# Joining the inverse of the delta rule: both steps' products spread over column places of the matrix engine, copied out by halves

## The chip, the cores and the metric

The kernel runs on one core of a Trainium2 chip. The metric is the device time of one execution in microseconds (us); the median of three runs of the kernel before is 1582.2 us (1581.89 to 1582.7). TensorE (PE in the profile, PEld for its weight loads), VectorE (DVE), ScalarE (ACT), GpSimd (POOL) and the queues of SyncE (SP) run side by side and wait for each other by semaphores.

## The reference, cut to what matters

One layer of a hybrid decoder: 256 tokens, model width 2048, a wide input projection, two branches (a gated delta rule with 32 value heads and an mLSTM with 8 heads), two output projections, a merge and an output product. The change concerns the delta rule alone. For each head and each chunk of tokens it solves a unit lower triangular system:

```python
    lower = jnp.where(strict, jnp.einsum('nbhid,nbhjd->nbhij', k_beta, kc) * decay, 0.0)
    unit_lower = lower + jnp.eye(CHUNK, dtype=f32)
    rhs = jnp.concatenate([v_beta, k_beta * jnp.exp(g_cum)[..., None]], axis=-1)
    sol = lax.linalg.triangular_solve(unit_lower, rhs, left_side=True, lower=True, unit_diagonal=True)
```

The kernel uses token blocks of 128 instead of chunks of 64, and applies the inverse of the 128x128 triangle to the right hand side.

## The kernel before, in words

**The stream.** `Stream.run` (L95) walks through all weights in pieces of 128x1024 numbers. A piece is cast by ScalarE into a high part (`whi`, L173), VectorE subtracts for the low part (`wlo`, L174), and TensorE multiplies both with the activations (L235, L628, L632). Up to three pieces are prepared ahead of their use (`ahead`, L67). After each piece used, `Side.step` (L46) lets every side job issue one step, in order of rank; a side job is a generator, and each `yield` in it hands back to the stream. So TensorE's program alternates between a piece of weights and what the side jobs add behind it. `side.debt` is a planner's account of VectorE time: a step takes off 1.6, jobs add their cost or give a credit where they put work on TensorE, and `side.room` (L53) holds the base inverse back while the account is too full.

**A period.** The delta rule has eight periods, `zg` 0 to 7 (`gdn_period`, L1039). Each one handles four heads with two token blocks each, so eight triangles of 128x128, numbered `m`, with m = 2 x head + token block. `base_inverse` (L815) inverts the 32x32 blocks on the diagonals on VectorE and puts them into `x0` (inverses by partition) and `y0` (their transposes); `xcmp` and `ycmp` hold them compactly, eight blocks side by side in each quarter of the partitions. `gdn_stage2` (L869) joins them. It starts 31 steps behind its period's scores (`STAGE2_STEPS`), while the next period's weights stream.

**The first step of the joining** (L879 to L906) makes 64x64 inverses from 32x32 ones. For each `m` and each half `t` of the triangle (partitions `r` = 64t and `o` = 64t + 32) one 32x32 product goes into the bank `mp` (L886), is copied to `pc_` (L890), and a second product goes into `mx` (L897, L900): two for the lower half (the block and its transpose), one for the upper half. Copies with the sign turned take them to `y0` (L902) and `x0` (L905).

**The second step** (L908 to L950) does the same from 64 to 128, for eight `m`: `first` (L911) makes 64x64 products from partitions 0 to 63 into partitions 64 to 127 of the bank `mq`, which are copied to `p2` (L924, L933); `second` (L914) multiplies from partitions 64 to 127 into partitions 0 to 63 of the bank `mz`, copied to `x0` (L932, L949). It is issued in three side steps: the four even `m` of `first`; then the four odd `m` of `first` alternating with the four even of `second`; then, behind the four products `pa` (L944) that apply the even blocks' inverse, the four odd `m` of `second`.

**What follows**: `pa`, `pb`, `pc` and `po` (L944, L956, L966, L974 to L977) apply the inverse and form the outputs.

**Places.** A product reads its two operands from some partitions (its rows in the array) and writes to some partitions of a PSUM bank (its columns in the array). A product of 32 or 64 rows and columns takes only a part of the 128x128 array, which is called its place here; its row place is where its operands lie, its column place is where its output lies. PSUM banks are handed out in turn by `gtile` (L206), four of them for all side jobs; a job waits for the next one with `banks`.

Of the kernel before, what the change touches and what calls it, by code (L numbers as in the profile page):

```python
# [9 lines left out]
AF = mybir.ActivationFunctionType  # L10
# [5 lines left out]
P = 128  # L16
S = 256
# [101 lines left out]
def hybrid_layer_kernel(  # L119
# [25 lines left out]
    V, A, T, G, SP = nc.vector, nc.scalar, nc.tensor, nc.gpsimd, nc.sync  # L145
# [60 lines left out]
    def gtile(nm, held=False):  # L206
        i = slots[0] % 4
        slots[0] += 1
        t = pg.tile([P, 512], F32, name=nm, tag="g")
        freed[i] = 1 << 30 if held else side.t + 1  # L210
        slots[1][id(t)] = i, t
        return t

    def gfree(t):
        freed[slots[1].pop(id(t))[0]] = side.t

    def banks(n):

        while any(freed[(slots[0] + j) % 4] >= side.t for j in range(n)):
            yield  # L220
# [16 lines left out]
    side = Side()  # L237
# [468 lines left out]
    def wait(n):  # L706
        for _ in range(n):
            yield
# [106 lines left out]
    def base_inverse(zg, res, zr):  # L815
# [49 lines left out]
        while zg < 7 and side.t < res["t"] + STAGE2_STEPS - 1:  # L865
            yield
        side.add(gdn_stage2(zg, res, zr), 0)

    def gdn_stage2(zg, res, zr):  # L869

        au, xc, yc = [res["au", z] for z in range(2)], res["xcmp"], res["ycmp"]

        def um(m):
            return au[m // 4][:, m % 4 // 2, 256 + 384 * (m % 2):384 + 384 * (m % 2)]

        def cols32(t, n=0):
            return t[:, n:n + 256].rearrange("p (m i) -> p m i", m=8)

        pc_ = bp.tile([P, 8, 32], F32, name="pcm", tag="pcm", bufs=1)  # L879
        yield from banks(2)  # L880
        pss = [gtile(f"mp{t}", True) for t in range(2)]
        side.debt -= 0.6
        for m in range(8):
            for t in range(2):
                r, o = 64 * t, 64 * t + 32
                T.matmul(pss[t][o:o + 32, m * 32:(m + 1) * 32], um(m)[r:r + 32, o:o + 32], yc[r:r + 32, m],  # L886
                         start=True, stop=True)
        for t in range(2):
            o = 64 * t + 32
            A.copy(pc_[o:o + 32], cols32(pss[t])[o:o + 32])  # L890
            gfree(pss[t])
        yield
        yield from banks(2)
        psx = [gtile(f"mx{t}", True) for t in range(2)]
        side.debt -= 0.6
        for m in range(8):
            T.matmul(psx[0][32:64, S + m * 32:S + (m + 1) * 32], xc[32:64, m], pc_[32:64, m], start=True, stop=True)  # L897
            for t in (1, 0):
                r, o = 64 * t, 64 * t + 32
                T.matmul(psx[t][r:r + 32, m * 32:(m + 1) * 32], pc_[o:o + 32, m], xc[o:o + 32, m],  # L900
                         start=True, stop=True)
        A.activation(y0[32:64, :, 0:32], cols32(psx[0], S)[32:64], AF.Copy, scale=-1.0)  # L902
        for t in range(2):
            r = 64 * t
            A.activation(x0[r:r + 32, :, r + 32:r + 64], cols32(psx[t])[r:r + 32], AF.Copy, scale=-1.0)  # L905
            gfree(psx[t])  # L906
        yield from wait(1 + (zg == 6))
        p2 = bp.tile([P, 8, 64], F32, name="p2", tag="p2", bufs=1)  # L908

        def first(ps, j, m):  # L910
            T.matmul(ps[64:128, j * 64:(j + 1) * 64], um(m)[0:64, 64:128], y0[:, m], start=True, stop=True)  # L911

        def second(ps, j, m):
            T.matmul(ps[0:64, j * 64:(j + 1) * 64], p2[64:128, m], x0[64:128, m, 64:128], start=True, stop=True)  # L914

        def part64(ps, r, o):
            return ps[r:r + 64, o:o + S].rearrange("p (m i) -> p m i", m=4)

        yield from banks(1)
        psp = gtile("mq", True)  # L920
        side.debt -= 0.5
        for j in range(4):
            first(psp, j, 2 * j)
        A.activation(p2[64:128, 0:8:2], part64(psp, 64, 0), AF.Copy, scale=-1.0)  # L924
        yield
        yield from banks(1)
        psz = gtile("mz", True)
        side.debt -= 0.5
        for j in range(4):
            first(psp, 4 + j, 2 * j + 1)  # L930
            second(psz, j, 2 * j)
        A.copy(x0[0:64, 0:8:2, 64:128], part64(psz, 0, 0))  # L932
        A.activation(p2[64:128, 1:8:2], part64(psp, 64, S), AF.Copy, scale=-1.0)  # L933
        gfree(psp)
        yield

        rr = res["rr"].rearrange("p b z (h d) -> p b (z h d)", h=2)
# [1 line left out]
        heads = [(g, g // 2, g % 2, slice(g * P, (g + 1) * P)) for g in range(4)]  # L939
        yield from banks(1)  # L940
        pa = gtile("pa", True)
        side.debt -= 1.3
        for g, z, h, c in heads:
            T.matmul(pa[:, c], x0[:, 2 * g], rr[:, 0, c], start=True, stop=True)  # L944
        for j in range(4):
            second(psz, 4 + j, 2 * j + 1)
        A.copy(ys[:, 0], pa)
        gfree(pa)
        A.copy(x0[0:64, 1:8:2, 64:128], part64(psz, 0, S))  # L949
        gfree(psz)  # L950
        yield from wait(2)
        yield from banks(1)
        pb = gtile("pb", True)
# [583 lines left out]
```

## Time and profile before

| | |
|---|---|
| median of 3 runs | 1582.2 us (1581.89 to 1582.7) |
| the profiled execution's own time | 1583.33 us |
| its span, first to last instruction | 1581.6 us |
| PE busy | 1565.7 us (99%) |
| PEld busy | 1315.6 us (83%) |
| DVE busy | 1159.7 us (73%) |
| ACT busy | 967.2 us (61%) |
| POOL busy | 249.7 us (16%) |
| DMA | 372.22 MB, mean 235 GB/s |
| granted clock of TensorE | 0.998 |

Busy time is the time in which at least one instruction of the engine was under way. In the timeline rows that are shown below, the columns are the start in us, the length in us of the merged row, the engine, the line, the operation, output <- inputs, rows*columns of the array, the shape, the number of records, and in brackets how long the engine was idle ahead of it and what released it. A float32 product shows as two records of its line: the sixteen products of L886 in a period are `x32`. Records overlap, since products are pipelined, so a cost is read from the start of a row to the start of the next one.

### The profile page before, as it was taken

Reading aid. Unit: us, or ns where it says so; the run is one execution under the profiler, and the core shown is the slowest. Engines: PE = TensorE matmul, PEld = TensorE weight load, DVE = VectorE, ACT = ScalarE, POOL = GpSimd, SP = SyncE. Lnnn points to the kernel's source line nnn. Section 1 sums busy time; section 2 is a strip of 40 time slices with the busy share of each in tenths; the row PEclk is TensorE's granted clock in tenths of the full one; section 3 lists DMA queues with packets and bytes.
Section 4 is the critical chain, followed back from the end, with each engine's and each line's share of the span. In section 5 each row is a group of like instructions: output and inputs, shape, how many; then the busy total and the mean of one; then the engine's idle time right before and its main releaser. Section 6 shows DMA issues by size and latency. Waiting matters only on the chain.

```text
span 1581.6 us, 23140 instructions
## 1 busy us (share of the span) xinstructions
PE 1565.7 (99%) x8574; PEld 1315.6 (83%) x8574; DVE 1159.7 (73%) x1884; ACT 967.2 (61%) x1608; POOL 249.7 (16%) x204
## 2 busy tenths in 40 slices
PE   8999999999999999999999999999999999999997
PEld 5888888888888888888888888888888888888886
DVE  6785556865789887988887988775868766756654
ACT  7754446765666676767676776766666554544443
POOL 4787761000000000000000000000000000100100
PEclk9999999999999999999999999999999999999999
DMA  9998775975565646575656565647878878766572
GB/s 379 392 385 334 267 288 188 288 245 193 182 195 175 209 147 202 167 201 168 202 167 198 172 199 171 199 142 247 281 270 314 339 264 298 282 237 237 213 269 107
DMA packets 167739, 372.22 MB, mean 235 GB/s; under 512 B 26021, under 2 KB 127797, under 8 KB 140105
## 3 DMA queue, kind: packets, MB, share of 16 engines
q1 hardware_dynamic: 167240, 370.13, 67.6%
q8 instruction: 67, 1.10, 0.3%
q10 hardware_dynamic: 290, 0.53, 0.1%
q14 instruction: 46, 0.38, 0.1%
q0 software_dynamic: 96, 0.09, 0.0%
HBM read 354.40 MB, written 16.31 MB: 234 GB/s over the span
## 4 chain that ended last, share of the span: by engine, by line
PE 81%; issue 13%; ACT 2%; DMA 1%; DVE 1%; POOL 1%; DVEq 0%; SPq 0%; ACTq 0%; POOLq 0%
PE pn L235 36%; PE pt L628 19%; PE pt L632 9%; PE py L235 8%; POOL mg L1327 1%; ACT whi L173 1%; DMA ya<-o_dr 1%; PE psa L235 1%; PE mq L911 1%; PE csil L305 0%; PE po L977 0%; PE pc L966 0%; PE po L976 0%; PE po L974 0%; PE pb L956 0%
## 5 line engine op out<-in xcount | busy, mean ns | idle before, releaser
L174 DVE TENSOR_TENSOR wlo<-raw,whi 128x1024 fp32r<-128x1024 f32 x453 | 556.1, 1235 | 241.1 <-ACT whi L173 240.2
L173 ACT CAST whi<-raw 128x1024 fp32r<-128x1024 f32 x516 | 532.1, 1046 | 261.3 <-PE pn L235 133.2
L235 PE MATMUL pn<-whi,h 128*128 128x512 f32 x1792 | 563.7, 392 | 0.9 <-ACT part L478 0.6
L628 PE MATMUL pt<-h,whi 128*128 128x512 f32 x1280 | 408.5, 400 | 0.0
L235 PEld LDWEIGHTS pn<-whi,h 128*128 128x128 f32 x1792 | 336.4, 188 | 71.9 <-ACT part L478 1.5
L235 PE MATMUL pn<-wlo,h 128*128 128x512 f32 x896 | 349.1, 390 | 0.9 <-POOL wlo L174 0.9
L632 PEld LDWEIGHTS pt<-h,wlo 128*128 128x128 f32 x1280 | 240.4, 188 | 56.6
L632 PE MATMUL pt<-h,wlo 128*128 128x256 f32 x1280 | 252.1, 278 | 0.0
L235 PEld LDWEIGHTS pn<-wlo,h 128*128 128x128 f32 x896 | 168.4, 188 | 35.4 <-POOL wlo L174 1.7
L628 PEld LDWEIGHTS pt<-h,whi 128*128 128x128 f32 x1280 | 195.4, 189 | 2.4
L174 POOL TENSOR_TENSOR wlo<-raw,whi 128x1024 fp32r<-128x1024 f32 (+1 forms) x63 | 145.7, 2320 | 51.6 <-ACT whi L173 51.6
L235 PE MATMUL py<-whi,yhi 128*128 128x512 f32 x384 | 150.8, 393 | 0.0
L235 PE MATMUL py<-whi,ylo 128*128 128x512 f32 x384 | 149.7, 390 | 0.0
L235 PE MATMUL py<-wlo,yhi 128*128 128x512 f32 x384 | 149.4, 389 | 0.0
L173 ACT CAST yhi<-ya 128x512 fp32r<-128x512 f32 x48 | 29.9, 622 | 130.3 <-PE py L235 114.9
L476 DVE TENSOR_TENSOR part<-pn,part 128x512 f32<-128x512 f32 x112 | 73.7, 685 | 45.2 <-PE pn L235 45.0
L719 POOL TENSOR_SCALAR_AFFINE_SELECT dd<-gb 128x256 f32<-128x256 f32 x40 | 25.9, 668 | 422.8 <-DMA gb<-rows 330.3
L174 DVE TENSOR_TENSOR ylo<-ya,yhi 128x512 fp32r<-128x512 f32 x48 | 33.2, 691 | 74.9 <-ACT yhi L173 72.2
L235 PEld LDWEIGHTS py<-whi,yhi 128*128 128x128 f32 x384 | 72.1, 188 | 15.6 <-ACT vt L1144 0.4
L235 PEld LDWEIGHTS py<-whi,ylo 128*128 128x128 f32 x384 | 72.1, 188 | 15.1
L235 PEld LDWEIGHTS py<-wlo,yhi 128*128 128x128 f32 x384 | 72.1, 188 | 14.9
L686 DVE SCALAR_TENSOR_TENSOR qs<-ab,gcv,qs 128x255 f32<-128x255 f32 (+2 forms) x192 | 81.0, 477 | 0.0
(263 smaller groups left out, 1612.9 us busy)
## 6 DMA issues: line engine op xcount, KB each, us to landing
raw<-in_dram SPq DMA_DIRECT2D x259, 1024.0 KB
ar<-in_dram SPq DMA_DIRECT2D x31, 1024.0 KB
raw<-in_dram SPq DMA_DIRECT2D x16, 512.0 KB
ya<-o_dr SPq DMA_DIRECT2D x32, 256.0 KB
gate_dr<-part SPq DMA_DIRECT2D x11, 512.0 KB
gb<-rows SPq DMA_DIRECT2D x20, 256.0 KB
raw<-in_dram SPq DMA_DIRECT2D x6, 768.0 KB
ug<-ud SPq DMA_DIRECT2D x32, 128.0 KB
```

Of the source, the lines that this page charges most:

```text
L173: A.copy(hi, src)
L174: (eng or V).tensor_tensor(lo, src, hi.bitcast(F32), op=ALU.subtract)
L235: T.matmul(ps, l, r, start=start and i == 0, stop=stop and i == 2, skip_group_check=True)
L476: V.tensor_tensor(part[g][:, b], ps[b], part[g][:, b], op=ALU.add)
L628: T.matmul(ps, hi[:, o:o + P], h2[:, k].rearrange("p a s -> p (a s)"), start=k == 0, stop=k == KC - 1, skip_group_check=True)
L632: T.matmul(ps[:, 0:S], lo[:, o:o + P], h_hi[:, k], start=False, stop=k == KC - 1, skip_group_check=True)
L686: V.scalar_tensor_tensor(dst[:, n, sh:], ab[i][:, 0:S - sh], taps(n, 3 - sh), dst[:, n, sh:], op0=ALU.mult, op1=ALU.add)
L719: G.affine_select(dd[:, :, blk * S:blk * S + P], gb[:, :, blk * P:(blk + 1) * P], pattern=[[0, 2], [1, P]], compare_op=ALU.is_ge, fill=-1e ...
L911: T.matmul(ps[64:128, j * 64:(j + 1) * 64], um(m)[0:64, 64:128], y0[:, m], start=True, stop=True)
L1327: G.tensor_tensor(mcols(b, hf, cg), mcols(b, hf, cg), s_, op=ALU.add)
```

## The change

In the first step, the products of the two token blocks of a head (`i` = 0 and 1, with m = 2j + i) now go to different column places. For `mp`, the even `m` keep the column place `o`, the odd `m` take `r`. For `mx`, the three products of an `m` take column places 32, 64 and 0 for even `m` and 96, 0 and 64 for odd `m`. Products with equal row places share a bank, as before. A bank's columns are then filled half as far, and every copy out becomes two: one for each `i`, of 32 x 128 numbers, which takes every second `m` of the destination (`sides`).

In the second step the three issues become two: `both` issues all eight products of `first` into one bank at column places 64 (even) and 0 (odd), and one side step later all eight of `second` into one bank at column places 0 (even) and 64 (odd). Each is copied out by two copies of 64 x 256 numbers, as many and as large as before. The odd half behind `pa` is gone. The planner's credits change with it: 0.6 for each of the two, and 0.8 at `pa`, where 0.5, 0.5 and 1.3 stood.

```diff
+        sides = slice(0, 8, 2), slice(1, 8, 2)
+
+        def fours(t, r, n=0):
+            return t[r:r + 32, n:n + P].rearrange("p (m i) -> p m i", m=4)
...
-        for m in range(8):
-            for t in range(2):
-                r, o = 64 * t, 64 * t + 32
-                T.matmul(pss[t][o:o + 32, m * 32:(m + 1) * 32], um(m)[r:r + 32, o:o + 32], yc[r:r + 32, m],
-                         start=True, stop=True)
+        for j in range(4):
+            for i in range(2):
+                m = 2 * j + i
+                for t in range(2):
+                    r, o = 64 * t, 64 * t + 32
+                    T.matmul(pss[t][(o, r)[i]:(o, r)[i] + 32, j * 32:(j + 1) * 32], um(m)[r:r + 32, o:o + 32],
+                             yc[r:r + 32, m], start=True, stop=True)
         for t in range(2):
-            o = 64 * t + 32
-            A.copy(pc_[o:o + 32], cols32(pss[t])[o:o + 32])
+            r, o = 64 * t, 64 * t + 32
+            for i in range(2):
+                A.copy(pc_[o:o + 32, sides[i]], fours(pss[t], (o, r)[i]))
             gfree(pss[t])
...
-        for m in range(8):
-            T.matmul(psx[0][32:64, S + m * 32:S + (m + 1) * 32], xc[32:64, m], pc_[32:64, m], start=True, stop=True)
-            for t in (1, 0):
-                r, o = 64 * t, 64 * t + 32
-                T.matmul(psx[t][r:r + 32, m * 32:(m + 1) * 32], pc_[o:o + 32, m], xc[o:o + 32, m],
-                         start=True, stop=True)
-        A.activation(y0[32:64, :, 0:32], cols32(psx[0], S)[32:64], AF.Copy, scale=-1.0)
+        for j in range(4):
+            for i in range(2):
+                m = 2 * j + i
+                for t, o, c, n, l, x_ in ((0, 32, (32, 96)[i], S, xc, pc_), (1, 96, (64, 0)[i], 0, pc_, xc),
+                                          (0, 32, (0, 64)[i], 0, pc_, xc)):
+                    T.matmul(psx[t][c:c + 32, n + j * 32:n + (j + 1) * 32], l[o:o + 32, m], x_[o:o + 32, m],
+                             start=True, stop=True)
+        for i in range(2):
+            A.activation(y0[32:64, sides[i], 0:32], fours(psx[0], (32, 96)[i], S), AF.Copy, scale=-1.0)
         for t in range(2):
             r = 64 * t
-            A.activation(x0[r:r + 32, :, r + 32:r + 64], cols32(psx[t])[r:r + 32], AF.Copy, scale=-1.0)
+            for i in range(2):
+                A.activation(x0[r:r + 32, sides[i], r + 32:r + 64], fours(psx[t], ((0, 64), (64, 0))[t][i]),
+                             AF.Copy, scale=-1.0)
             gfree(psx[t])
...
+        def both(nm, outs, operands):
+
+            ps = gtile(nm, True)
+            side.debt -= 0.6
+            for j in range(4):
+                for i, o in enumerate(outs):
+                    T.matmul(ps[o:o + 64, j * 64:(j + 1) * 64], *operands(2 * j + i), start=True, stop=True)
+            return ps, [ps[o:o + 64, 0:S].rearrange("p (m i) -> p m i", m=4) for o in outs]
 
         yield from banks(1)
-        psp = gtile("mq", True)
-        side.debt -= 0.5
-        for j in range(4):
-            first(psp, j, 2 * j)
-        A.activation(p2[64:128, 0:8:2], part64(psp, 64, 0), AF.Copy, scale=-1.0)
+        ps, views = both("mq", (64, 0), lambda m: (um(m)[0:64, 64:128], y0[:, m]))
+        for v, m in zip(views, sides):
+            A.activation(p2[64:128, m], v, AF.Copy, scale=-1.0)
+        gfree(ps)
         yield
         yield from banks(1)
-        psz = gtile("mz", True)
-        side.debt -= 0.5
-        for j in range(4):
-            first(psp, 4 + j, 2 * j + 1)
-            second(psz, j, 2 * j)
-        A.copy(x0[0:64, 0:8:2, 64:128], part64(psz, 0, 0))
-        A.activation(p2[64:128, 1:8:2], part64(psp, 64, S), AF.Copy, scale=-1.0)
-        gfree(psp)
+        ps, views = both("mz", (0, 64), lambda m: (p2[64:128, m], x0[64:128, m, 64:128]))
+        for v, m in zip(views, sides):
+            A.copy(x0[0:64, m, 64:128], v)
+        gfree(ps)
         yield
...
-        side.debt -= 1.3
+        side.debt -= 0.8
...
-        for j in range(4):
-            second(psz, 4 + j, 2 * j + 1)
         A.copy(ys[:, 0], pa)
         gfree(pa)
-        A.copy(x0[0:64, 1:8:2, 64:128], part64(psz, 0, S))
-        gfree(psz)
```

More of the change, by code (lines that the diff above doesn't have):

```diff
@@ L874, in um @@
             return au[m // 4][:, m % 4 // 2, 256 + 384 * (m % 2):384 + 384 * (m % 2)]
-        def cols32(t, n=0):
-            return t[:, n:n + 256].rearrange("p (m i) -> p m i", m=8)
+        sides = slice(0, 8, 2), slice(1, 8, 2)
+        def fours(t, r, n=0):
+            return t[r:r + 32, n:n + P].rearrange("p (m i) -> p m i", m=4)
         pc_ = bp.tile([P, 8, 32], F32, name="pcm", tag="pcm", bufs=1)
@@ L908, in gdn_stage2 @@
         p2 = bp.tile([P, 8, 64], F32, name="p2", tag="p2", bufs=1)
[L910 to L917, printed above, removed]
-        yield from banks(1)
-        psp = gtile("mq", True)
-        side.debt -= 0.5
-        for j in range(4):
-            first(psp, j, 2 * j)
-        A.activation(p2[64:128, 0:8:2], part64(psp, 64, 0), AF.Copy, scale=-1.0)
+        def both(nm, outs, operands):
[5 more added lines that the diff above has]
+            return ps, [ps[o:o + 64, 0:S].rearrange("p (m i) -> p m i", m=4) for o in outs]
+        yield from banks(1)
+        ps, views = both("mq", (64, 0), lambda m: (um(m)[0:64, 64:128], y0[:, m]))
+        for v, m in zip(views, sides):
+            A.activation(p2[64:128, m], v, AF.Copy, scale=-1.0)
+        gfree(ps)
         yield
         yield from banks(1)
-        psz = gtile("mz", True)
-        side.debt -= 0.5
-        for j in range(4):
-            first(psp, 4 + j, 2 * j + 1)
-            second(psz, j, 2 * j)
-        A.copy(x0[0:64, 0:8:2, 64:128], part64(psz, 0, 0))
-        A.activation(p2[64:128, 1:8:2], part64(psp, 64, S), AF.Copy, scale=-1.0)
-        gfree(psp)
+        ps, views = both("mz", (0, 64), lambda m: (p2[64:128, m], x0[64:128, m, 64:128]))
+        for v, m in zip(views, sides):
+            A.copy(x0[0:64, m, 64:128], v)
+        gfree(ps)
         yield
```

## The prediction, made before the changed kernel had run

> **What bounds the kernel now.** I read the page first, then TensorE's waits, then the windows of one period, then TensorE's timeline of the joining in period `zg` = 1 (600 to 632 us), and last ScalarE's timeline there and in the last two periods.
>
> ```profile
> span 1581.6 us, 23140 instructions
> ```
>
> ```profile
> PE csil L305 <- ACT ar L303: 4.5, 1, 4.5
> PE mpt L1127 <- ACT oT L1019: 1.0, 1, 1.0
> ```
>
> ```profile
> 600.00:680.00 80.00, 80.00 (x545) 69.20 (x544) 68.42 (x146) 56.50 (x112) 6.36 (x9) 1.00 0.59 181
> ```
>
> The first row is the page's head. The next two are the longest of six in the answer on TensorE's waits; none of the six is a wait of the joining's products, and only the second falls into the periods. The window's columns are PE, PEld, DVE, ACT and POOL busy, granted clock, DMA share and GB/s: TensorE is busy for 80.00 of 80 us at full clock, VectorE for 68.42, ScalarE for 56.50. So TensorE's program runs without holes through the periods, and what is cut from it comes off the end, as long as VectorE (11.6 us free per 80) and ScalarE (23.5 us) stay ahead. I therefore cost the change by TensorE's starts: from the first product of a block to the first product of what follows.
>
> ```profile
> 600.50 0.69 PE L886 MATMUL mp<-ycmp,au 32*32 32x32 f32 x32
> 601.12 0.73 PE L628 MATMUL pt<-h,whi 128*128 128x512 f32 x2
> ```
>
> ```profile
> 604.11 0.21 PE L897 MATMUL mx<-pcm,xcmp 32*32 32x32 f32 x1
> 604.11 0.22 PE L900 MATMUL mx<-xcmp,pcm 32*32 32x32 f32 x2
> 604.16 0.19 PE L897 MATMUL mx<-pcm,xcmp 32*32 32x32 f32 x1
> 604.16 0.20 PE L900 MATMUL mx<-xcmp,pcm 32*32 32x32 f32 x2
> ...
> 604.60 0.19 PE L897 MATMUL mx<-pcm,xcmp 32*32 32x32 f32 x1
> 604.61 0.20 PE L900 MATMUL mx<-xcmp,pcm 32*32 32x32 f32 x2
> 604.74 0.73 PE L628 MATMUL pt<-h,whi 128*128 128x512 f32 x2
> ```
>
> **First step, what the places do now.** The `mp` block takes 601.12 - 600.50 = 0.62 us. Its 16 products are 32 records in two places (rows 0 to 31 and rows 64 to 95), so 16 records in each place. The merged row is 0.69 long and one record takes 0.19 (the rows of single records below it), so the last starts 0.50 behind the first: 16 rounds of 31 ns, and 0.12 us to the next work. The `mx` block takes 0.63: 24 products, 48 records, in three places. From 604.16 to 604.60 the L897 rows come 15 times, so 14 rounds of 31 ns, each with three records. Three records a round cost no more than two, though two of the three (L897 and one of the L900) read the same rows, 32 to 63, and differ only in their columns, 32 and 0. That is the case that the change makes everywhere: equal rows, other columns.
>
> - `mp` after: four places (rows 0 and 64, two columns each), 8 rounds of 31 ns: **-0.25 us**. Bounds: 0 (no more overlap than now) and -0.25.
> - `mx` after: six places (four columns on rows 32 to 63, two on rows 96 to 127), 8 rounds. Here the rate at which records can start may bind. In the row of 604.16 the two L900 records together take 0.20, one of them 0.191 (the median in the tile view below), so the second starts some 7 ns (estimate; rounding leaves 4 to 10) behind the first. Six records then need 42 ns a round, not 31: 8 x 42 = 0.34 in place of 0.50, **-0.16 us**. Bounds: 0 and -0.25.
>
> The Trainium skill ("TensorE: Matmul & The Clock Gate", Part 3, Measured speedup vs the span model) gives about 4 ns per further tile; by it six records fit in a round, `mx` would gain 0.25 and the total would be 0.7 us better than the sum below. No run here shows six places.
>
> ```profile
> L900 PE MATMUL mx<-xcmp,pcm x256: 190/191/213, 524.0 to 1066.2; 32*32 32x32 f32 x128
> L890 ACT COPY pcm<-mp x16: 362/364/367, 521.6 to 1065.2; 32x256 f32<-32x256 f32 x16
> L985 ACT ACTIVATE junk<-po x64: 273/277/288, 558.1 to 1102.0; 128x128 f32<-128x128 f32 x64
> ```
>
> ```profile
> 607.72 0.68 PE L911 MATMUL mq<-y,au 64*64 64x64 f32 x8
> 608.33 0.73 PE L628 MATMUL pt<-h,whi 128*128 128x512 f32 x2
> ```
>
> ```profile
> 611.32 0.27 PE L911 MATMUL mq<-y,au 64*64 64x64 f32 x1
> 611.33 0.27 PE L914 MATMUL mz<-x,p 64*64 64x64 f32 x1
> ...
> 611.93 0.73 PE L628 MATMUL pt<-h,whi 128*128 128x512 f32 x2
> ```
>
> ```profile
> 614.84 1.05 PE L944 MATMUL pa<-rr,x 128*128 128x128 f32 x8
> 615.82 0.68 PE L914 MATMUL mz<-x,p 64*64 64x64 f32 x8
> 616.43 0.72 PE L628 MATMUL pt<-h,whi 128*128 128x512 f32 x2
> ```
>
> ```profile
> 623.82 1.05 PE L956 MATMUL pb<-ys,au 128*128 128x128 f32 x8
> 624.63 0.70 PE L628 MATMUL pt<-h,whi 128*128 128x512 f32 x2
> ```
>
> **Second step.** The block of four `first` alone (8 records in one place) takes 608.33 - 607.72 = 0.61 us; the mixed block (16 records in two places) takes 611.93 - 611.32 = 0.61 as well. So a second place is free here too, though these two differ in rows and columns. The third block stands behind `pa`: from `pa` to the weights 616.43 - 614.84 = 1.59, while the like block `pb`, without anything behind it, takes 624.63 - 623.82 = 0.81. So the third block costs 0.78, of which 0.17 is the second change of the array's shape.
>
> After the change there are two blocks of 16 records in two places: 0.61 each if equal rows with other columns overlap as the `mx` rounds show, and the 0.78 is gone: **-0.78 us**. Bounds: if the two places go one after the other, each block gets 8 more records. One record in one place costs (0.68 - 0.27)/7 = 0.06 us (the merged row of 607.72, less the length of one record as in the row of 611.32, over seven steps). Two blocks then lose 2 x 8 x 0.06 = 0.96, and the step comes out 0.18 worse than now. I take full overlap, by the `mx` rounds.
>
> **ScalarE's copies.** `pc_` gets four copies of 128 columns for two of 256, `y0` two for one, `x0` four for two: five instructions more per period. The copy of 256 took 0.364; the nearest row with 128 columns took 0.277 (128 partitions, with a sum), so a half costs between 0.18 (half) and 0.36 (no cheaper); I take 0.28. Per period 10 x 0.28 - 5 x 0.38 = +0.9 us of ScalarE, 7 us in all, under its 23.5 free in 80. `p2` and `x0` in the second step have as many copies as before. What matters is whether a product waits:
>
> ```profile
> 602.19 0.75 ACT L890 COPY pcm<-mp 32x256 f32<-32x256 f32 x2
> ...
> 605.26 0.76 ACT L905 ACTIVATE x<-mx 32x256 f32<-32x256 f32 x2
> ...
> 608.43 0.38 ACT L924 ACTIVATE p<-mq 64x256 f32<-64x256 f32 x1 [1.33 <-PE mq L911]
> ...
> 612.08 0.37 ACT L932 COPY x<-mz 64x256 f32<-64x256 f32 x1 [2.19 <-PE mz L914]
> ```
>
> ```profile
> 1003.93 0.75 ACT L890 COPY pcm<-mp 32x256 f32<-32x256 f32 x2
> 1004.77 0.21 PE L897 MATMUL mx<-pcm,xcmp 32*32 32x32 f32 x1
> ```
>
> ```profile
> 1064.78 0.75 ACT L890 COPY pcm<-mp 32x256 f32<-32x256 f32 x2
> 1065.65 0.21 PE L897 MATMUL mx<-pcm,xcmp 32*32 32x32 f32 x1
> ```
>
> In `zg` 1, and by the regular timeline in 0 to 5, `pc_` is ready at 602.94 and needed at 604.11. After: ready at 602.19 + 4 x 0.28 = 603.31, needed at 603.86 (0.25 earlier). Even at 0.38 each it is 603.71. `x0` ends at 606.02, later by 0.9: ahead of 607.72. The new waits: `mz` now waits for both halves of `p2` (608.43 + 2 x 0.4 = 609.2, needed 611.3), and `pa` for both of `x0` (612.08 + 0.8 = 612.9, needed 614.8), both with 2 us of weight products as cover; without it the queued weights would lose that much. No DMA moves and no queue of SP or POOL is passed.
>
> In the last two periods that cover is gone. `zg` 6: `pc_` ends at 1004.68, `mx` starts at 1004.77. After, the copies end 0.35 later, and `mp`'s 0.25 is waited away: +0.35. `zg` 7: the same +0.35 at 1065.65, and the 1.0 us wait of `mpt` for `oT` (the waits' row above), which stands behind `pc_` on ScalarE, eats what `mx` gains.
>
> The planner's credit falls from 2.3 to 2.0 per period. At worst the base inverse, hence the joining, comes a side step later; the weights that fill TensorE are the same, so I cost it at nothing, with +-0.5 us in the last two periods.
>
> **The sum.** `zg` 0 to 5: 0.25 + 0.16 + 0.78 = 1.19, six times: -7.1. `zg` 6: -0.16 - 0.78 + 0.35 = -0.6. `zg` 7: -0.78 + 0.35 = -0.4. Together -8.1 us. The profiled execution took 1583.33 us (span 1581.6 and 1.7 around it), so 1575.2; against the median of 1582.2, which is 1.1 lower, 1574.1.
>
> **The rivals.**
>
> 1. *The 32-wide products gain nothing* (records can't start faster, or loads for equal rows queue): only the second step counts, 8 x -0.78 + 0.7 = -5.5: 1576.7, and 1577.6 with halves at full price. For it: 48 records in 0.50 us is the densest that the trace shows, and the change asks for more. Against: `mp` has only 32 in that time, and has room up to `mx`'s rate.
> 2. *Equal rows don't overlap at all.* The second step is 0.18 worse, the first stays, copies cost 0.7: 8 x 0.18 + 0.7 = +2.1: 1584.3, no measurable difference. Against it: the three records of an `mx` round. The Trainium skill (same page and part, The mechanism) says that a weight load overlaps products under way only where the row group differs. By that rule this rival is what happens, since every pair that the change makes has equal rows; the trace disagrees for 32-wide places and shows no 64-wide pair.
> 3. *Slower: each change of column place on equal rows costs what a change of shape costs.* From the rows of `pa`, 0.78 - 8 x 0.06 = 0.30 us for two changes, 0.15 each. With 32 records a period in the second step, each behind such a change: 32 x 0.15 = 4.8 against 1.2 saved, +3.6 a period: +29 us, 1611. It decides from 1.19/32 = 37 ns a record on. Against it: in `mx` column 32 and column 0 alternate on equal rows at 31 ns a round. For it: only that 64-wide was never seen.
> 4. *VectorE or ScalarE becomes the bound*: per period 68.4 of 78.8 us for VectorE, no.
>
> **How the numbers follow.** Forecast 0.77 (1574.1, from 1571.7 with `mx` at its bound and no late copies to 1576.1 with `mx` at 0 and halves at full price); rival 1 0.10; rival 2 0.09; rival 3 0.04. The range from 1571.7 to 1577.7 takes in the forecast's bounds and rival 1, and leaves out 0.13. A measurement of this kernel can tell 0.2%, 3.2 us, from no change: faster is below 1579.0 (forecast and rival 1: 0.87), the same 0.09 (rival 2), slower 0.04 (rival 3).
>
> **What would show it.** In the changed profile: `mp` block to the weights 0.37 us, `mx` 0.47 (0.38 if starts don't bind, 0.63 if nothing overlaps), `mq` and `mz` with 16 records each in 0.61, `pa` to the weights 0.81; the period 600.50 to 680.64 about 1.2 shorter; a wait of `mx` for `pcm` in the last two periods of 0.3 to 0.6. Wrong would be `mq` at 1.1 (rival 2) or beyond 3 (rival 3), or TensorE waits for `wlo` or `whi` in the periods.

## The result and the profile after

The changed kernel is slower: 1592.13 us, median of 4 runs (1590.54 to 1594.53), against 1582.45 of the kernel before, a ratio of 1.0062 (95% interval 1.0047 to 1.0077). The forecast was 1574.1. The profiled execution took 1590.54 us, its span is 1588.8: 7.2 us more than before, where 8.1 us less was worked out.

The products did what was forecast. TensorE's timeline in the changed kernel, period `zg` = 1 (columns as before):

```profile
599.44 0.45 PE L890 MATMUL mp<-ycmp,au 32*32 32x32 f32 x32
599.83 0.74 PE L628 MATMUL pt<-h,whi 128*128 128x512 f32 x2
...
602.81 0.21 PE L906 MATMUL mx<-pcm,xcmp 32*32 32x32 f32 x1
...
603.01 0.19 PE L906 MATMUL mx<-pcm,xcmp 32*32 32x32 f32 x1
603.05 0.25 PE L906 MATMUL mx<-xcmp,pcm 32*32 32x32 f32 x3
...
603.22 0.21 PE L906 MATMUL mx<-xcmp,pcm 32*32 32x32 f32 x2
603.36 0.73 PE L628 MATMUL pt<-h,whi 128*128 128x512 f32 x2
...
606.34 0.68 PE L925 MATMUL mq<-y,au 64*64 64x64 f32 x16
606.96 0.73 PE L628 MATMUL pt<-h,whi 128*128 128x512 f32 x2
...
609.95 0.68 PE L925 MATMUL mz<-x,p 64*64 64x64 f32 x16
610.57 0.50 PE L235 MATMUL psa<-qh 128*128 128x512 f32 x1
...
615.17 1.05 PE L948 MATMUL pa<-rr,x 128*128 128x128 f32 x8
615.98 0.70 PE L628 MATMUL pt<-h,whi 128*128 128x512 f32 x2
...
622.97 1.16 PE L956 MATMUL pb<-ys,au 128*128 128x128 f32 x8 [1.18 <-ACT ys L949]
...
630.76 1.16 PE L966 MATMUL pc<-rr,x 128*128 128x128 f32 x8 [1.02 <-DVE rr L959]
```

`mp` takes 0.39 us (0.37 forecast), `mx` 0.55 (0.47), `mq` 0.62 and `mz` 0.62 with 16 records each (0.61), `pa` 0.81 (0.81). What was not forecast is the row behind `mz`: `psa`, the scores of the next period's first pair of heads, comes straight behind it, ahead of `pa`. Before, it came one block of weights behind `pa` and the last `mz`, whose rows at 614.84 and 615.82 the prediction shows:

```profile
619.31 0.40 PE L235 MATMUL psa<-qh 128*128 128x512 f32 x1
```

And `pb` and `pc` now wait, with two reasons in the brackets: ScalarE's copy of `pa` and VectorE's subtraction.

The windows of the changed kernel from one `mp` to the next, `zg` 0 to 5 (length, then TensorE, its loads, VectorE, ScalarE, GpSimd busy):

```profile
520.43:599.44 79.01, 79.01 (x545) 68.36 (x544) 67.68 (x146) 56.38 (x116) 7.03 (x9) 1.00 0.56 175
599.44:681.24 81.80, 79.60 (x546) 68.52 (x545) 68.08 (x146) 56.42 (x117) 7.17 (x9) 1.00 0.57 177
681.24:761.97 80.73, 79.73 (x545) 68.64 (x545) 68.05 (x146) 56.97 (x117) 6.92 (x9) 1.00 0.59 181
761.97:842.97 81.00, 79.94 (x545) 68.74 (x545) 68.06 (x146) 56.98 (x117) 7.09 (x9) 1.00 0.59 181
842.97:924.74 81.77, 80.01 (x546) 68.71 (x545) 68.18 (x146) 56.93 (x117) 6.97 (x9) 1.00 0.59 178
924.74:1007.99 83.25, 80.68 (x545) 68.48 (x545) 69.65 (x149) 56.79 (x116) 7.96 (x12) 1.00 0.59 178
```

Two periods of the kernel before:

```profile
520.36:600.50 80.14, 80.14 (x545) 69.31 (x545) 67.97 (x147) 56.14 (x112) 6.40 (x9) 1.00 0.57 178
600.50:680.64 80.14, 80.14 (x545) 69.30 (x545) 68.43 (x147) 56.64 (x112) 6.36 (x9) 1.00 0.59 181
```

The first period is 1.13 us shorter, with TensorE busy all the time, close to the 1.19 of the sum. The next five are 81.80, 80.73, 81.00, 81.77 and 83.25 long instead of that 79.01: 13.5 us lost. These 13.5 less six gains of 1.13 are the 6.7 us by which the six periods grew. TensorE, 100% busy before, is idle 2.2 us in the second period, while the busy time of VectorE and ScalarE there fell by 0.4 and 0.2 us and GpSimd's rose by 0.8. So most of it is waiting, not work: over the five periods TensorE is idle for 8.6 of the 13.5 us. A wait inside a block can also count as busy: the `mx` block takes 1.0 us in `zg` 2 to 5 in place of 0.55, 1.9 us more in all. The other 3 us are not accounted for here.

Who waited for whom, in the changed kernel, over the whole span (us in total, times, longest):

```profile
PE pc L966 <- DVE rr L959: 5.1, 5, 1.1
...
PE pb L956 <- ACT ys L949: 1.9, 2, 1.2
```

```profile
POOL dd L719 <- DMA gb<-rows: 369.0, 17, 44.8
...
ACT dd L727 <- POOL dd L719: 55.0, 14, 5.9
```

The same two waits in the kernel before:

```profile
POOL dd L719 <- DMA gb<-rows: 330.3, 16, 44.9
...
ACT dd L727 <- POOL dd L719: 16.0, 9, 2.0
```

ScalarE waited 16.0 us for the decay mask `dd` before, and 55.0 us after. A period has two score stages, one per pair of heads. Before, 12 of the 16.0 us were waits of 2.0 in the second stage of `zg` 0 to 5, while the first stage's exponents found their mask ready. After, the first stage's exponents wait 1.9 to 5.9 us in each of these six periods, and the second's 3.6 to 4.2. The chain is followed in SyncE's queue, GpSimd and ScalarE around 610 us. The changed kernel:

```profile
606.08 5.38 SPq L712 DMA_DIRECT2D gb<-rows  x1
```

```profile
618.18 0.76 POOL L719 TENSOR_SCALAR_AFFINE_SELECT dd<-gb 128x256 f32<-128x256 f32 x2 [33.19 <-DMA gb<-rows]
```

```profile
611.45 1.28 ACT L727 ACT_TABLE_LOAD   x1
618.62 0.40 ACT L727 ACTIVATE dd<-dd,ngt 128x128 f32<-128x128 f32 x1 [5.89 <-POOL dd L719]
...
622.33 0.59 ACT L949 COPY ys<-pa 128x512 f32<-128x512 f32 x1
```

The kernel before:

```profile
606.30 4.21 SPq L712 DMA_DIRECT2D gb<-rows  x1
```

```profile
617.20 1.59 POOL L719 TENSOR_SCALAR_AFFINE_SELECT dd<-gb 128x256 f32<-128x256 f32 x2 [32.66 <-DMA gb<-rows]
```

```profile
615.93 0.59 ACT L947 COPY ys<-pa 128x512 f32<-128x512 f32 x1 [1.37 <-PE pa L944]
...
618.41 1.28 ACT L727 ACT_TABLE_LOAD   x1
619.70 0.40 ACT L727 ACTIVATE dd<-dd,ngt 128x128 f32<-128x128 f32 x1
```

The mask's rows are asked for at 606.08 and release GpSimd at 618.18, 12 us later; before, it was 606.30 and 617.20, and ScalarE copied `pa` ahead of the exponents, which then had nothing to wait for. Now ScalarE's exponents of the mask (L727) stand at the head of its queue from 611.45, right behind the scores that were issued early, and wait 5.89 us. Behind them stand the weight casts and the copy of `pa`, which TensorE left by 616 and which is copied at 622.33. That is `pb`'s wait. `pc` waits for VectorE's subtraction (L959), which needs `pb` and now stands behind VectorE's part of the early scores (L777, L788).

In the first period the scores are as early, but the mask's load was asked for at 526.26 and released GpSimd at 535.18, 8.9 us later. ScalarE waited 1.90 us, and TensorE lost nothing:

```profile
535.62 0.40 ACT L727 ACTIVATE dd<-dd,ngt 128x128 f32<-128x128 f32 x1 [1.90 <-POOL dd L719]
```

**Why the scores came early.** Stage 1 (L748) asks for three banks. Before, `mq` was given back one side step after its first products, and `mz` only behind `pa`; with four banks handed out in turn, stage 1 could not have its three until the step behind `pa`. The change gives each bank back in the step that fills it, so stage 1 finds its three two side steps earlier.

### The profile page after: what moved, and what is told of

The parts are those of the page before. It is cut to its first block, busy times and chain, and to the rows that moved or that the text cites. A ratio compares the mean times of both kernels' runs of the same rounds, so it can differ in the third digit from the quotient of the medians.

```text
span 1588.8 us, 23181 instructions
## 1 busy us (share of the span) xinstructions
PE 1563.3 (98%) x8574; PEld 1311.2 (83%) x8574; DVE 1158.7 (73%) x1884; ACT 971.2 (61%) x1648; POOL 254.9 (16%) x204
## 4 chain that ended last, share of the span: by engine, by line
PE 58%; issue 14%; DVE 12%; ACT 8%; DMA 6%; POOL 2%; SPq 0%; DVEq 0%; POOLq 0%; ACTq 0%
PE pn L235 30%; PE pt L628 9%; PE py L235 8%; DMA gb<-rows 5%; DVE wlo L174 5%; PE pt L632 5%; ACT whi L173 2%; DVE qs L686 2%; DVE au L788 1%; POOL dd L719 1%; POOL mg L1327 1%; DVE xx L844 1%; DVE ab L677 1%; DVE tmp L840 1%; PE csil L305 0%
## 5 line engine op out<-in xcount | busy, mean ns | idle before, releaser
L719 POOL TENSOR_SCALAR_AFFINE_SELECT dd<-gb 128x256 f32<-128x256 f32 x40 | 30.6, 787 | 440.8 <-DMA gb<-rows 369.0
```

What stands on the lines that cost most here:

```text
L719: G.affine_select(dd[:, :, blk * S:blk * S + P], gb[:, :, blk * P:(blk + 1) * P], pattern=[[0, 2], [1, P]], compare_op=ALU.is_ge, fill=-1e ...
```

## The experiments

Theory 1 is this order: early release, early scores, ScalarE blocked by a mask whose rows are not there. Theory 2: the five more ScalarE copies per period push its queue late. Theory 3: the planner's credits, or the paired places themselves. The kernel before had a median of 1582.27 to 1582.66 us in these comparisons.

**Held banks.** The change, with the releases of before:

```diff
-        gfree(ps)
         yield
         yield from banks(1)
+        gfree(ps)
         ps, views = both("mz", (0, 64), lambda m: (p2[64:128, m], x0[64:128, m, 64:128]))
...
-        gfree(ps)
         yield
...
         gfree(pa)
+        gfree(ps)
```

> The changed kernel, but the banks of the second step are given back as late as in the kernel before (mq one side step later, mz behind pa). Theory 1, order: the early release lets the next period's scores (psa) go out two side steps earlier; the exponents of their decay mask then stand at the head of ScalarE's queue while the mask still waits for its rows from DRAM, and the copies of pa and pc and the weight casts queue behind. Then this kernel has the gain of the products and not the loss: 1574.5 us (1572 to 1577). Theory 2, copies: the five more ScalarE copies a period push the queue late: still 1588 to 1593. Theory 3, the paired places slow TensorE: still 1588 to 1593.

Measured: 1576.21 us, ratio 0.9959 (0.9947 to 0.9972). All of the change's products and copies are in it, and two of its periods read

```profile
520.58:599.61 79.03, 79.03 (x546) 68.38 (x545) 68.23 (x147) 56.88 (x117) 6.72 (x9) 1.00 0.57 182
599.61:678.64 79.03, 79.03 (x546) 68.37 (x545) 68.40 (x147) 57.44 (x117) 6.30 (x9) 1.00 0.58 183
```

with ScalarE's wait for the mask back at

```profile
ACT dd L727 <- POOL dd L719: 16.3, 9, 2.1
```

The loss is gone in all six periods, so neither the copies nor the pairs caused it.

**Order alone.** The first step as before; the second step with the early releases of the change, all eight products in one column place (shown against the change's `both`):

```diff
-                    T.matmul(ps[o:o + 64, j * 64:(j + 1) * 64], *operands(2 * j + i), start=True, stop=True)
-            return ps, [ps[o:o + 64, 0:S].rearrange("p (m i) -> p m i", m=4) for o in outs]
+                    c = outs[0]
+                    T.matmul(ps[c:c + 64, i * S + j * 64:i * S + (j + 1) * 64], *operands(2 * j + i), start=True, stop=True)
+            return ps, [ps[c:c + 64, i * S:(i + 1) * S].rearrange("p (m i) -> p m i", m=4) for i in range(2)]
```

> The first step as before; the second step in two issues with the early release of the change, but all eight products of a step in one column place one after the other (no pairs; copies out by halves as before). TensorE's own work is about 0.15 us a period more than before (two blocks of 1.07 against 0.61 + 0.61 + 0.78). Theory 1, order alone: slower than before by the 15 us that the change lost against its sum, less what is hidden: 1592 to 1600 us. Theories 2 and 3 (copies of the first step, pairs): 1583 to 1585, since neither is in it.

Measured: 1591.16 us, ratio 1.0055 (1.0041 to 1.0068): a loss without any pair and without the first step's copies. It lies 0.8 us under the range that I gave, and it is a smaller loss than the change's: the second to sixth period are together 6.0 us longer than five times the first (80.25), not 13.5. `psa` starts later here (612.64), since the longer `mq` and `mz` stand ahead of it, and ScalarE waits 48.9 us for the mask in all. Its `mq` shows what eight products in one place cost:

```profile
607.50 1.14 PE L919 MATMUL mq<-y,au 64*64 64x64 f32 x16
608.57 0.73 PE L628 MATMUL pt<-h,whi 128*128 128x512 f32 x2
```

1.07 us, against 0.62 in two column places on equal rows: the pairs overlap.

**Second step alone**, the first step's code as before the change:

> Only the second step is changed, the first step is as before, so no copy is added. Theory 1: the scores still go early, so slower than before, by about the first step's worth more than the changed kernel: 1592 to 1597 us. Theory 2 (copies): 1577, the gain of the third block alone.

Measured: 1589.15 us, ratio 1.0038 (1.0024 to 1.0051). ScalarE waits 56.0 us for the mask, without a copy more than before. That refutes theory 2. The 1592 to 1597 expected was too high, 2.9 us at its lower end, and why stays open. In the two profiles the first six periods come out as expected: 489.6 us together here, 487.6 in the changed kernel, so 2.0 for the missing gain of the first step. From the last `mp` to the end it is the other way, 519.7 us here and 521.4 there, where TensorE runs at half its clock for 3.4 us (last section). The first step's copies do not explain it: with the planner's old credits (below) `mx` keeps its 0.55 us up to `zg` 4 and takes 0.57 in `zg` 5, and that kernel is as slow as the change.

**First step alone**, the second step's code as before:

> Only the first step is changed (products in more places, ten half copies a period for five); the second step, its releases and its credits are as before. Theory 1: 0.24 + 0.08 us of TensorE less a period and waits in the last two: 1580 to 1582 us. Theory 2 (copies): slower than before, 1586 or more.

Measured: 1582.64 us, ratio 0.9999 (0.9990 to 1.0008). Neither theory's number: no loss as theory 2 has it, and no gain. Its first period is 79.80 long against 80.14, so 0.34 a period are there. `mx` now waits in the last two periods (1.04 us in `zg` 6, and 2.30 up to the next work in `zg` 7, against 0.63 and 1.73 before), but in the profile that takes back 0.2 us in `zg` 6 only. The ten runs spread from 1580.6, the profiled one, to 1583.98; what the slower ones lost, and where, no trace shows.

**Rows of the mask early.** The change with its early scores; only the load moves, in the first of the two score stages:

```diff
         z = p % 2
+        if z == 0:
+            gb = decay_rows(2 * p)
         yield from conv_half(ps, gdn_taps(p), qs, 1, *((1, 0) if z else (3, 1)))
...
-        gb = decay_rows(2 * p)
+        if z:
+            gb = decay_rows(2 * p)
         dd = decay_mask(gb)
```

> The changed kernel with its early order as it is, but for the first of each two score stages (z = 0) the load of the mask's rows from DRAM is issued at the start of the stage, some nine side steps earlier. Theory 1a: what ScalarE waits for is the mask's rows (the load lands 12 us after its issue, 8 us behind the scores); then its 55 us of waits fall to some 10 or less and the time to 1574 to 1579 us, with the scores as early as in the changed kernel. Theory 1b: the early order costs by itself (three banks held earlier, VectorE's scores ahead of the subtraction that pc needs), whatever the mask does: 1585 or more.

Measured: 1579.27 us, ratio 0.9978 (0.9968 to 0.9987), 0.3 us over theory 1a's range and far from 1b's. ScalarE around 612 us, scores as early as in the change:

```profile
611.34 1.28 ACT L727 ACT_TABLE_LOAD   x1
612.63 0.40 ACT L727 ACTIVATE dd<-dd,ngt 128x128 f32<-128x128 f32 x1
```

No wait; `pa` is copied at 616.15 instead of 622.33. Of the 17.9 us between the change and the best kernel below, 12.9 come back with one DMA that starts earlier. About half of the rest lies in `zg` 5, still 81.23 us long, with an `mx` block of 1.18 us. One part of the expectation failed: ScalarE still waits 22.2 us for the mask, not some 10. All six of these waits, 3.6 to 4.2 us each, stand in the second score stage, and four of the six periods are within 0.12 us of 79.01 all the same. So the sum of the waits is not the cost; what counts is what stands behind each.

**Scores later.** The change with its early releases; the first score stage waits two side steps more:

```diff
-        yield from wait(2)
+        yield from wait(2 if z or p == 0 else 4)
         yield from banks(3)
         res["t"] = side.t
```

> The changed kernel with its early bank releases, but the first of each two score stages waits two side steps more ahead of its banks, which puts the scores back to where they were before. Theory 1: as with the held banks, 1574.8 to 1577.5 us; the bank is only the gate, the order is what costs. If holding the bank itself mattered: different from the held banks by more than 2 us.

Measured: 1574.43 us, ratio 0.9949 (0.9936 to 0.9963), periods of 79.03 again. That is 0.4 us under the range and 1.8 from the held banks, within the 2 us set. The bank was only the gate.

**Credits of before** (0.5, 0.5 and 1.3):

> The changed kernel with the planner's credits of before (0.5, 0.5 and 1.3 in place of 0.6, 0.6 and 0.8). Theory 3, the credits move the base inverse on VectorE and so the loss: 1574 to 1580 us. Theory 1: no matter, 1589 to 1595.

Measured: 1591.94 us, ratio 1.0058 (1.0044 to 1.0071). The credits don't matter for the time. The five periods behind the first are 13.5 us longer than five times the first here too, though `mx` takes 0.55 to 0.57 us in all of them.

**Scores early, exponents late.** The change, but what follows the scores on ScalarE and VectorE comes two side steps later:

```diff
+        if z == 0 and p:
+            yield from wait(2)
         decay_exp(dd, gb, ngt[:, 0, 2 * p:2 * p + 2], b12, ngt[:, 1, 2 * p:2 * p + 2])
```

> The changed kernel with the scores on TensorE as early as in it, but for z = 0 everything behind them on ScalarE and VectorE (the mask's exponents first) two side steps later, so that ScalarE's queue is not blocked while the mask's rows are on their way; three banks stay held for longer instead. Theory 1 in its exact form (the block at the head of ScalarE's queue is the loss): 1574 to 1580 us, like the early rows. If early scores on TensorE or held banks are the loss: 1586 or more.

Measured: 1577.69 us, ratio 0.9968 (0.9957 to 0.9979). The first five periods are 79.01 each, though TensorE does the scores as early as in the change; the sixth is 80.39. In ScalarE's queue the copy of `pa` is now ahead of the exponents:

```profile
615.68 0.59 ACT L951 COPY ys<-pa 128x512 f32<-128x512 f32 x1 [3.87 <-PE pa L950]
...
617.79 1.28 ACT L727 ACT_TABLE_LOAD   x1
619.08 0.40 ACT L727 ACTIVATE dd<-dd,ngt 128x128 f32<-128x128 f32 x1
```

So it is not the early scores on TensorE and not the held banks. This run also moves VectorE's part of the scores back; the early rows left it early and lost 0.1 us a period in three of the five. What the two runs share is that no instruction waits at the head of ScalarE's queue in front of the copy of `pa`: that wait is the greater part of the loss. What is left in the sixth period, 1.4 us here and 2.2 with the early rows, is not explained.

**The last two periods.** Held banks, and there the first step as before (`if zg > 5:` around the old code):

> The held banks, and in the last two periods the first step as before the change (whole copies). If the half copies there cost what the held-bank run's rows show (mx stretched by 0.47 us twice, and after it a stretch at half the clock of 3.4 us in some executions, 1.7 us), this gives 1573 to 1575 us against 1576.2 of the held banks alone. If not, 1575.5 to 1577.5.

Measured: 1574.76 us, ratio 0.9949 (0.9937 to 0.9962), 1.5 under the held banks alone. And with the later scores in place of the held banks:

> The two repairs together: the scores two side steps later (early releases kept) and the first step as before in the last two periods. If each does what its own run showed, 1572.5 to 1574.5 us, under the 1574.4 and 1574.8 of the two alone; if the half copies there cost nothing by themselves, as the later scores alone: 1574.4.

Measured: 1574.22 us, ratio 0.9945 (0.9933 to 0.9958), the best of all, but not to be told from 1574.43 with the half copies. So the copies in the last two periods cost about what the products gain there. The 1.5 us between the two held-bank kernels must then have another part; the last section has a candidate.

## Why the prediction was wrong

- *What bounds the kernel, and that a cut of TensorE's work comes off the end*: right. With the order restored, 1574.4 and 1576.2 us were measured with all of the change's products and copies, and 1574.1 was forecast. (The lower end of the range, 1571.7, does not come out of its terms: 8 x 1.28 off 1582.2 gives 1572.0.)
- *The second step, -0.78*: right (three blocks became two of 0.62, and `pa` costs 0.81). Equal rows with other columns overlap in 64-wide places too, so rival 2 and rival 3 are out. The rule of the Trainium skill ("TensorE: Matmul & The Clock Gate", Part 3, The mechanism), that a weight load overlaps products only on other row groups, disagrees with this: 0.62 us for 16 records on equal rows, 1.07 in one place.
- *The first step, -0.25 and -0.16*: `mp` -0.24, `mx` -0.08, 0.55 us for 48 records, halfway between the forecast and rival 1. The estimate of 7 ns a record was not what was off: the first 32 records start within 0.20 us (602.81 to 603.01 in the rows above), some 6 ns apart. The last 16 start between 603.05 and 603.24, some 13 ns apart. Why they are slower stays open.
- *ScalarE's copies*: 0.28 us each was right (from start to start), and so was it that they don't hurt in the first six periods: with the held banks these are 79.03 to 79.07 long.
- *The last two periods*: `zg` 6 came out as forecast, 59.34 us against 59.96, with the forecast wait in `mx` (1.01 us in place of 0.55). From the `mp` of `zg` 7 to the end -0.4 was forecast and 1.0 more was measured, 521.4 us against 520.4; the stretch at half the clock in the last section costs some 1.7 there.
- **The step that failed** is the list of new waits, closed with "No DMA moves and no queue of SP or POOL is passed". The sentence holds as far as it goes: the mask's load is asked for at 606.08 us, and at 606.30 before. But the work that needs it moved. The list followed the change's own instructions and their waits, and not what its earlier bank releases let go: they open `banks(3)` of another job, whose exponents then stand ahead of the copy of `pa` on ScalarE. That term was put at nothing without a reason; only the planner's credit was weighed ("so I cost it at nothing", rightly). It measured 13.5 us in five periods, and it turns the sign of the total.
- The row that gave it away is the first in the kernel before's list of waits: GpSimd waits 330.3 us in 16 turns for the mask's rows. In `zg` 1 GpSimd works on them from 617.20 to 618.79, and ScalarE's exponents start at 619.70. So there was 0.9 us to spare, and the scores came 7.7 us earlier, counted from `mp`. I weighed the waits of TensorE alone, since only its idle time costs.
- *Rival 4*, that VectorE or ScalarE becomes the bound, I dismissed by its share of busy time. Shares say nothing of a queue that is blocked at its head: ScalarE was some 70% busy in those periods (56.4 of 81.8 us in the second) and still late.

## What to carry to other kernels

When a change gives a buffer back earlier, ask who is waiting for that buffer, and walk through everything that this job issues, on every queue, up to the first thing that isn't ready yet. In a program that alternates by hand-written steps, a release is a scheduling decision. A saving is then checked by the order of the blocks, not by their durations: `mq`, `mz` and `pa` had the forecast lengths in every period here while the kernel lost.

## What the hardware showed beside

In the changed kernel's last period TensorE waits for `oT` and right behind it runs at half its clock:

```profile
1073.86 0.66 PE L1127 MATMUL mpt<-con,hn 128*128 128x128 f32 x4 [1.18 <-ACT oT L1019]
```

```profile
1074.70:1078.10 3.40, 3.40 (x13) 2.92 (x12) 0.17 (x1) 3.11 (x8) 0.00 (x0) 0.50 1.04 352
```

The granted clock is 0.50 for 3.4 us, which costs about 1.7 (an estimate: half of 3.4). The profiles of the held banks, the old credits and the late exponents show the same stretch; the other three with half copies in the last two periods don't, and none of the five kernels (the one before among them) with whole copies there does. In the seven with half copies `mx` takes some 0.9 us in that period, with a wait of 0.46 inside it. The Trainium skill ("TensorE: Matmul & The Clock Gate", Part 1, HAM oscillation) names idle gaps above some 3.4 us as what to avoid; the gap in the row above is 1.18, and the three profiles without the stretch have the same one. What decides whether the stretch comes stays open. It may be behind the spread of the held banks: their two slowest runs (1577.44 and 1577.14) have a granted clock of 0.997, the other three 0.998 or 0.999. That is not shown, and neither is a part of it in the first step alone.
